# Rolling rows by DMA: the order of the wrapped row ends on GpSimd's ring

## The chip, the cores and the metric

One core of a Trainium2 chip runs the kernel. The metric is the device time of one execution in microseconds (us). The profile is of one execution. Its granted TensorE clock was 1.0, and TensorE does nothing. A run is marked slow when it is over 1.5% above the fastest of the same kernel; with one core and no clock change, that mark only tells how far a run lies from the fastest. Ratios are the mean time of one kernel's fast runs over that of the other's fast runs of the same rounds, so they are not quite the ratio of the medians that are quoted beside them.

## The reference

```python
x = np.random.randn(8192, 8192).astype(np.float32)   # shift = 100
def reference(x, shift):
    return np.roll(x, shift, axis=1)
```

A row has 32 KiB. Of each row, 8,092 elements (32,368 B, "the body") move 100 places to the right, and the last 100 (400 B, "the wrap") go to the front.

## The kernel before

```python
engines = [nc.sync, nc.scalar]
n_chunks = 16
rows = n_rows // n_chunks                  # 512
for i in range(n_chunks):
    r = slice(i * rows, (i + 1) * rows)
    engines[i % 2].dma_start(out=out[r, s:], in_=x[r, :n_cols - s])
    if s > 0:
        nc.gpsimd.dma_start(out=out[r, :s], in_=x[r, n_cols - s:])
# ... launch: one core, x and out in HBM
```

There is no SBUF and no compute: SyncE and ScalarE issue the body in 16 DMAs, GpSimd issues the wraps in 16 DMAs.

## Time and profile before

| | before |
|---|---|
| median of 4 runs | 844.44 us (841.96 to 846.6) |
| wrap packets (queue q0, without completions) | 768, mean 347 ns, 31 over 1 us |
| body packets (q1 and q10) | 8,192, mean 1,590 ns |
| time of all data packets over 16 engines | 830.8 us |
| last packet ends, from the start of the trace | 840.7 us |

The last four rows are from the packet records of the trace. In these records 97.6% of the data packets start within 5 ns of where another one ended, and 16 are under way at once for 750 of the 838.5 us from the first to the last. So I take it that an engine handles one packet at a time without gaps, and the sum of packet times over 16 is then the time that evenly loaded engines would need. The prediction shows the lines of the page.

### The profile page before, as it was taken

To read this page: it belongs to the slowest core of one execution; us is meant where nothing else is said; L and a number is where in the kernel's file an instruction comes from. 1 tells how busy PE (TensorE), PEld (TensorE's weight loads), DVE (VectorE), ACT (ScalarE), POOL (GpSimd) and SP (SyncE) were. 2 spreads that over 40 slices of the span, in tenths; PEclk is the share of its full clock that TensorE was granted. 3 is DMA by queue.
4 is the path that set the end of the run, shared out by engine and by line. 5 is a ranking of instruction groups with operands and counts; after the bars stand their busy time and mean duration, and the time that the engine had idled before them with its cause. 6 is when DMAs were issued, how large, how long until landed. Compare 5 with 4: busy or idle time off the path is not lost. (4 is left out here: it accounts for less than half of the span.)

```text
span 841.9 us, 81 instructions
## 1 busy us (share of the span) xinstructions
POOL 10.2 (1%) x20
## 2 busy tenths in 40 slices
POOL 2000000000000000000000000000000000000000
DMA  9999999999999999999999999999999999999996
GB/s 286 312 315 332 311 322 312 309 315 325 314 332 315 320 321 320 332 326 321 323 323 328 323 321 324 320 321 324 331 328 317 331 324 324 328 332 317 323 331 220
DMA packets 9472, 268.44 MB, mean 319 GB/s; under 512 B 512, under 2 KB 512, under 8 KB 1280
## 3 DMA queue, kind: packets, MB, share of 16 engines
q1 hardware_dynamic: 4224, 132.58, 49.0%
q10 hardware_dynamic: 4224, 132.58, 47.7%
q0 software_dynamic: 1024, 3.28, 2.0%
HBM read 268.44 MB, written 268.44 MB: 638 GB/s over the span
## 5 line engine op out<-in xcount | busy, mean ns | idle before, releaser
L30 POOL DMA_DIRECT2D out_dram<-in_x_dram x16 | 10.0, 630 | 109.5 <-DMA out_dram<-in_x_dram 108.7
L47 POOL MEMSET const-bfloat16-1.0<- 128x1 bf16 x1 | 0.1, 102 | 0.0
L47 POOL MEMSET const-float32-0.0<- 128x1 f32 x1 | 0.1, 99 | 0.2 <-issue 0.2
L47 POOL MEMSET const-float32-1.0<- 128x1 f32 x1 | 0.1, 99 | 0.0
L47 POOL MEMSET const-uint8-127<- 128x1 uint8 x1 | 0.1, 99 | 0.0
## 6 DMA issues: line engine op xcount, KB each, us to landing
out_dram<-in_x_dram ACTq DMA_DIRECT2D x8, 16184.0 KB, 400.1
out_dram<-in_x_dram SPq DMA_DIRECT2D x8, 16184.0 KB, 401.1
out_dram<-in_x_dram POOLq DMA_DIRECT2D x16, 200.0 KB, 112.8
```

Source lines behind the costliest of these rows:

```text
L30: nc.gpsimd.dma_start(out=out[r, :s], in_=x[r, n_cols - s:])
L47: nc = _bacc.Bacc("TRN2", target_bir_lowering=False, num_devices=1)
```

## The change

The intent: consecutive descriptors on GpSimd's ring should not lie on neighbouring rows but 4 rows apart. The body is untouched, and so is the number of wrap DMAs.

```diff
         engines[i % 2].dma_start(out=out[r, s:], in_=x[r, :n_cols - s])
-        if s > 0:
-            nc.gpsimd.dma_start(out=out[r, :s], in_=x[r, n_cols - s:])
+    if s > 0:
+        xt = x.rearrange("(k e m q) c -> k q e m c", k=4, e=16, q=4)
+        ot = out.rearrange("(k e m q) c -> k q e m c", k=4, e=16, q=4)
+        for k in range(4):
+            for q in range(4):
+                nc.gpsimd.dma_start(out=ot[k, q, :, :, :s], in_=xt[k, q, :, :, n_cols - s:])
```

## The prediction

> **What bounds the kernel now.** The kernel only moves bytes: HBM to HBM, 256 MiB read and as much written. So I read the page's second and third parts first, which show how full the 16 DMA engines are and which queue fills them.
>
> ```profile
> span 841.9 us, 81 instructions
> ...
> DMA  9999999999999999999999999999999999999996
> ...
> q1 hardware_dynamic: 4224, 132.58, 49.0%
> q10 hardware_dynamic: 4224, 132.58, 47.7%
> q0 software_dynamic: 1024, 3.28, 2.0%
> HBM read 268.44 MB, written 268.44 MB: 638 GB/s over the span
> ```
>
> The engines are at least nine tenths busy in every slice but the last, where they finish a little apart. The two body queues (SyncE's q1 and ScalarE's q10) take 96.7% of the engines' time, and GpSimd's ring q0, the only thing the change touches, takes 2.0%. That is 0.020 x 842 = 16.8 us of the span for 1.2% of the bytes.
>
> Next I asked whether that 16.8 us is really on the path. The busy time by stretches, with the stretch in which the wraps move (6 to 231 us, from the packet records) and the stretch after it:
>
> ```profile
> core 0: us, POOL busy (x), PEclk, DMA share, GB/s
> 6.00:231.00 225.00, 5.27 (x9) 1.00 1.00 315
> 231.00:820.00 589.00, 0.00 (x0) 1.00 1.00 324
> ```
>
> The engines are full in both (share 1.00), but move 315 GB/s while wraps are mixed in and 324 without. From the packet records: body packets (32,368 B each, 8,192 of them) pass at 9.29 per us in the first stretch and 10.02 per us in the second. So (10.02 - 9.29) x 224.5 = 164 body packets were displaced, which at 10.02 per us is 16.4 us. Two ways of counting agree: the wraps cost about 16.5 us of wall time. The mean duration of a body packet is 1.59 us in both stretches, so wraps take their own time and do not visibly slow the body. If I sort the packets into 16 chains in which each packet starts where another ended, over 95% fit to within 5 ns: an engine handles one packet at a time with no gaps, and the chains end between 831 and 841 us.
>
> Last the waits, to see whether any order between instructions matters:
>
> ```profile
> engine line waited for: us in total, times, longest us
> POOL out_dram L30 <- DMA out_dram<-in_x_dram: 108.7, 8, 15.0
> ```
>
> GpSimd waits 8 times, once for each wrap DMA after the first eight, for an earlier one to land; its last issue is at 119 us and the last wrap packet moves at 231 us. All of it lies 600 us before the end. The instruction chain of the page ends in an unknown queue and names nothing useful here; the bound is the sum of packet times on 16 engines.
>
> [...] The trace shows 512 packets of 4,400 B and 256 of 4,000 B[...] and I expect the same cut after. [...]
>
> **The change part by part.**
> - The body's 16 DMAs keep their queues, order, shapes and rows: 8,192 packets of a mean 1.59 us, 13,025 us of engine time, over 16 engines 814 us. Change: 0.
> - The wraps stay 16 DMAs of 512 x 400 B from GpSimd, 0.63 us of issue each (10.0 us in all, hidden). 768 data packets stay 768. Change in counts: 0.
> - What moves is only the address order. [...] The issue stands behind all body issues in the program text, but GpSimd runs its own stream, so that shifts nothing.
>
> So the whole effect is 768 x (change of a wrap packet's duration) / 16. Today's mean is 267 us / 768 = 347 ns, with a clear shape: 463 of 768 packets (60%) take 185 ns or less, with the fastest at 171 ns for 4,400 B and 155 ns for 4,000 B; the other 40% form a tail up to 1.5 us. If all ran at the fastest: (512 x 171 + 256 x 155) / 16 = 8.0 us. So of 16.7 us, 8.0 us are a floor that no order of rows removes, and 8.7 us are a tail. 171 ns for 4,400 B is 25.7 GB/s on an engine, close to the fastest body packet's 32,368 B / 1,196 ns = 27.1 GB/s. So at 32 KiB pitch a packet can already run at an engine's full pace, and the pitch by itself is not what makes the tail. The tail looks like meeting other traffic: body packets too have a fastest time of 1.20 us and a mean of 1.59. That meeting does not depend on whether the wraps are 1 or 4 rows apart. I choose a mean of 300 to 450 ns after, that is -2.3 to +4.9 us, [...] centre 365 ns, +0.9 us on 845.8.
>
> **Rivals.**
> - *The order removes the tail.* For it: 40% of packets have one, and the change must have been made for something. Against: the floor packets already lie at the same pitch. Best case -8.7 us, 837 us. Even this is 1.0%; 2% (16.9 us) would need wraps that cost nothing.
> - *The pitch hurts.* [...] Against: [...] here in the first 231 us only 1.19 of 16 engines are on a wrap packet at a time (267 / 224.5)[...]. If it doubles the mean to 694 ns: +16.7 us, 862 us, just at 2%. For slower by over 2% the mean must pass 700 ns.
> - *New waits.* The strided pattern of the wraps could be taken by the framework as overlapping the body's writes, and the wraps would wait for body DMAs. The last four (the last 2,048 rows) would then run after the end, one after the other. Against: in before, body and wraps interleave in the same address range too, and no wait between them is in the list, so rows are told apart finely. Estimate 10 to 25 us more, 856 to 870 us. I give it 5%. Waits of wraps for one another alone would be hidden by 600 us of slack.
>
> **Range and chances.** Runs of before spread over 3.5 us. The centre is 846.5 us. The likely band of packet durations gives 843 to 851; the spread of runs, half of the first rival below and a part of the second above widen it to 839 to 857. Faster by over 2% (below 829) has no mechanism: 1%. Slower by over 2% (above 863) needs the doubled packet or new waits: 7%. Within: 92%.
>
> **What would show it.** Right: again 9,472 packets, q0 between 1.7% and 2.6% of the engines' time, body packets at 1.59 us, GB/s about 315 early and 324 late, POOL x16 at about 0.63 us. The tail rival: q0 near 1.0% and nearly all packets under 185 ns. The pitch rival: q0 near 4% and the 171 ns packets gone. New waits: GpSimd waiting hundreds of us, and q0 packets at the end. I am wrong altogether if body packets, which the change does not touch, change their mean duration, or if the wrap DMAs lose engines or are cut into other packets.

## The result, and the profile after

The changed kernel took 869.32 us (median of 4 runs, 865.85 to 884.24; the last is marked slow) beside 844.44. The ratio is 1.0282, with a 95% interval from 1.0223 to 1.0341: slower. The prediction's range ended at 857.

The page of the changed kernel, its span, DMA share by slice, and queues with packets, MB and share of the engines' time:

```profile
span 864.1 us, 81 instructions
...
DMA  9999999999999999999999999999999999999951
...
q10 hardware_dynamic: 4224, 132.58, 46.6%
q1 hardware_dynamic: 4224, 132.58, 46.5%
q0 software_dynamic: 1024, 3.28, 3.5%
```

The numbers of packets and bytes are the same as before. Two things are new. The wraps' share went from 2.0% to 3.5%. And the engines are not full to the end: the last two slices read 5 and 1, where before only the last one read 6. The busy time by stretches shows both (columns: stretch, its length, POOL busy, clock, mean busy share of the DMA engines, GB/s):

```profile
6.00:231.00 225.00, 5.26 (x9) 1.00 1.00 309
231.00:820.00 589.00, 0.00 (x0) 1.00 1.00 323
820.00:864.00 44.00, 0.00 (x0) 1.00 0.41 162
```

The same view of before, for its end:

```profile
820.00:842.00 22.00, 0.00 (x0) 1.00 0.64 224
```

While the wraps move, the kernel is now at 309 GB/s and not 315; afterwards it is as fast as before, 323 beside 324. At the end, the engines are on average only 41% busy for 44 us: some have finished and wait for others.

The packet records give the sum. Wraps: mean 624 ns and not 347, which is 768 x 277 ns / 16 = 13.3 us more. Body: mean 1,572 ns and not 1,590, which is 8,192 x 18 ns / 16 = 9.2 us less. That gain is not spread over the run: from 6 to 231 us, while the wraps move, the body's mean fell from 1,594 to 1,533 ns, after 820 us, when some engines have finished, it is 1,299 and was 1,486, and in between it is as before (1,597 beside 1,592). Body packets ran faster just when other engines were held up by wraps or idle. So the time of all data packets over 16 engines rose from 830.8 to 834.9 us, by 4.1 us only. But the last packet ended at 862.7 us and not 840.7. The gap between the even load and the last engine went from 9.9 to 27.8 us. That is 18 of the 22 us.

When the gap arises is shown by the 4-byte packets. There are 256 of them in the two body queues, 16 for each DMA, and in the trace of before 256 semaphore updates of these DMAs follow them by 0.3 to 1.5 us; so I read them as the reports of completion, one from each engine. For ScalarE's second body DMA the first and last engine reported at 215.3 and 237.0 us before, and at 207.3 and 265.7 us after, a spread of 58 us. Before, the spread at the second DMA was 22 us. In the changed kernel most of it stays to the end: for the last DMA it is 41 us, and was 10 before.

GpSimd's waits are of the same kind as before, so no new order between instructions came in:

```profile
POOL out_dram L36 <- DMA out_dram<-in_x_dram: 126.7, 8, 18.7
```

### The profile page after: what moved, and what is told of

Read it like the earlier page. It is cut to its first block, busy times and chain, and to the rows that moved or that the text cites.

```text
span 864.1 us, 81 instructions
## 1 busy us (share of the span) xinstructions
POOL 10.2 (1%) x20
## 2 busy tenths in 40 slices
DMA packets 9472, 268.44 MB, mean 311 GB/s; under 512 B 512, under 2 KB 512, under 8 KB 1280
## 3 DMA queue, kind: packets, MB, share of 16 engines
q0 software_dynamic: 1024, 3.28, 3.5%
```

## The experiments

Each kernel was timed beside the kernel before on the same chip; before's median on these chips was 841.6 to 851.5 us. Wherever packets are counted below, it is from the packet records of the profiled run. "Long" is a wrap packet over 1 us: 31 of 768 before, 189 after.

The theories in the expectations speak of a pitch "between engines" and one "inside a packet". There I assumed that each of 16 engines takes 32 consecutive rows of a DMA's list. No packet record names its engine or its rows, so this was my assumption and is not shown; the distances in the theories are what I believed. The last section of the experiments comes back to it, because it leaves a riddle. Each diff shows only the lines that matter, against the kernel that they were taken from (before or the changed one), with the omitted lines left out.

### Which part of the order: neighbouring rows in 128-row blocks

```diff
-xt = x.rearrange("(k e m q) c -> k q e m c", k=4, e=16, q=4)          # likewise ot
+xt = x.rearrange("(k e q m) c -> k q e m c", k=4, e=16, q=4, m=32)    # likewise ot
```

> Right result. [...] Theory P (pitch inside a packet): the 128 KiB steps make wrap packets slow; then this runs like before, 842 to 848 us, with a mean wrap packet near 347 ns and engines that end within some 10 us of each other. Theory E (pitch between engines): the 4 MiB between the 16 engines does it; then this runs like the changed kernel, 865 to 872 us, with packets near 620 ns and ends 40 us apart. Theory B (both add): in between, some 855 us and 480 ns.

Measured: 867.02 us, ratio 1.0293 (1.0187 to 1.0398), right result. The time and the ends of the engines (39 us apart) are those of theory E, and the packets are those of theory P: mean 319 ns, 41 long. So it is neither. The stretches of this kernel and of before show a third thing:

```profile
2.00:22.00 20.00, 4.37 (x8) 1.00 1.09 194
22.00:44.00 22.00, 0.63 (x1) 1.00 1.00 227
44.00:120.00 76.00, 3.15 (x5) 1.00 1.00 284
```

```profile
2.00:22.00 20.00, 4.91 (x8) 1.00 1.05 323
22.00:44.00 22.00, 0.62 (x1) 1.00 0.99 307
44.00:120.00 76.00, 3.73 (x6) 1.00 1.00 319
```

The first fence is this kernel, the second is before. Here the body is slowed from the start and recovers over 120 us. The first 16 wrap packets, which leave from 6.3 us on, took 2,445 ns on average (368 before, 1,291 in the changed kernel), and the 32 body packets that started next took 3,730 ns (1,610 before, 1,455 in the changed kernel). This jolt does not exist in the changed kernel. The experiment shows that the same loss of time can come about in two ways, and that a time alone does not tell which.

### No wraps

```diff
-    if s > 0: ...                        # all wrap DMAs removed; wrong result on purpose
```

> Wrong result on purpose: no wraps at all. Gives the cost of the wraps in both kernels. If wraps cost their mean engine time: before minus 16.7 us, about 828 us. If the body alone has its engines level, they end within 5 us of each other, where they ended within 10 us before and 41 us after, and the unevenness is due to the wraps. Rival: the engines are uneven by themselves (20 us or more apart), and the wraps only sum with it.

Measured: 821.09 us, ratio 0.9769 (0.9695 to 0.9842). The wraps cost before 0.0231 x 841.6 = 19.4 us, by the interval 13 to 26, so this agrees with the 16.7 us of their engine time. The body alone leaves the engines 18 us apart at its last DMA, so they are uneven by themselves: my second expectation (5 us) failed, and its rival (20 us or more) is nearly right. But the body's own unevenness grows slowly (5 us at the first DMA, 8 at the second), while the changed kernel has 58 us at the second. Most of the unevenness of the changed kernel comes with the wraps.

### Reads or writes

```diff
+on = out.rearrange("(i e m) c -> i e m c", i=16, e=16)          # neighbouring rows, as before
-... dma_start(out=ot[k, q, :, :, :s], in_=xt[k, q, :, :, n_cols - s:])
+... dma_start(out=on[4 * k + q, :, :, :s], in_=xt[k, q, :, :, n_cols - s:])   # wrong rows on purpose
```

> Wrong rows on purpose: the wraps read in the changed kernel's order and write in the order of before. If the slow side is the reads: about 868 us and wrap packets near 620 ns. If it is the writes: about 845 us and near 350 ns. If each gives half: about 856 us.

Measured: 837.75, 850.53, 864.47 and 877.95 us; only the lowest counts as fast, so there is no ratio. The profiled run is the slowest one: 174 long packets, mean 565 ns, and at the last DMA two engines reported at 873.6 and 874.8 us while the other fourteen were done by 822.8. The end of its DMA line and its wrap queue:

```profile
DMA  9999999999999999999999999999999999998211
...
q0 software_dynamic: 1024, 3.28, 3.1%
```

The long packets are here with the reads alone, and in this run the unevenness too. But the one fast run, at 837.75 us, is no slower than before, and no trace of it was kept. So the effect of the reads alone on the time is not shown.

The mirror, with reads as before and writes in the changed kernel's order:

```diff
+xn = x.rearrange("(i e m) c -> i e m c", i=16, e=16)
+... dma_start(out=ot[k, q, :, :, :s], in_=xn[4 * k + q, :, :, n_cols - s:])   # wrong rows on purpose
```

> Wrong rows on purpose: the wraps read in the order of before and write in the changed kernel's order. The mirror of the run that reads 4 apart: about 868 us and 620 ns if the writes are the slow side, about 845 us and 350 ns if the reads are, about 856 us if each gives half.

Measured: 839.73 us, ratio 1.0025 (0.9921 to 1.0130), mean 343 ns, 17 long. The order of the writes makes no long packets by itself, and no harm to the time is seen (the interval leaves room for 1.3%). The order of the reads makes the long packets.

### The wraps alone, without the body

```diff
-    for i in range(n_chunks): ...        # body removed, wraps kept; wrong result on purpose
```

> Wrong result on purpose: the wraps of before alone, no body. Theory of meeting: a wrap packet is slow only because the body is beside it; then packets run near their floor, 171 ns, in this order and in the changed order alike. Rival: the order is slow by itself; then this shows a mean near 200 ns and the changed order one of 600 ns or more.

> Wrong result on purpose: the changed kernel's wraps alone, no body. Order slow by itself: mean packet over 600 ns, with packets of 1.5 to 3 us as beside the body. Slow only in meeting the body: near 171 ns, the same as the order of before alone.

Measured: 33.35 us in the order of before and 48.53 us in the changed order (one run each). Span and the wraps' queue, first of the order of before, then of the changed one:

```profile
span 31.6 us, 61 instructions
...
q0 software_dynamic: 1024, 3.28, 76.7%
```

```profile
span 46.8 us, 61 instructions
...
q0 software_dynamic: 1024, 3.28, 84.6%
```

The mean packet was 496 ns and 812 ns, with no long packet in the first and 197 in the second. The changed order is slow by itself, with no body to meet: both expectations for the order of before (171 and 200 ns) failed, but the changed order's 600 ns or more came true. It also shows that 171 ns is no typical pace of the old order: with nothing but other wraps beside them, packets took 496 ns on average.

### Is the jolt of the first experiment due to the start?

```diff
+for q in range(4): nc.gpsimd.dma_start(out=ob[0, q, :, :, :s], in_=xb[0, q, :, :, n_cols - s:])   # 128-row blocks
-for i in range(16): ...                  # order of before
+for i in range(4, 16): ...
```

> Right result. [...] Theory of the start: in the run with all sixteen like that, the first round of wrap packets, which all engines send at once at 6.3 us, took 1 to 3 us each and threw the body into packets of 5 us that recover over 120 us; so four such DMAs at the start do all the harm, about 865 us. Rival: the harm goes with the number of such DMAs: 842 + 4/16 x 25, about 848 us.

Measured: 877.97 us, ratio 1.0318 (1.0244 to 1.0391). First 16 wrap packets 2,669 ns, next 32 body packets 3,811 ns. Four such DMAs at the start do as much harm as sixteen. With the four last instead (chunks 0 to 11 in the order of before, then block 3):

> Right result. The mirror: twelve wrap DMAs as before[...]. Theory of the start: like before, 840 to 846 us. Rival (harm by number): about 848 us; if a late collision throws the body too, 855 us or more.

Measured: 859.14 us, ratio 1.0090 (1.0055 to 1.0124), so not free, as the theory of the start had it, but a third of the harm; 848/842 of the rival is 1.007. The start explains most of the first experiment's loss, and not all.

### Reads alone: 4 rows apart at the old block size, and neighbouring rows in blocks of 128

```diff
+src = bass.AP(x.tensor, offset, [[32 * n_cols, 16], [4 * n_cols, 32], [1, s]])   # rows 32e + 4m, wrong rows on purpose
+nc.gpsimd.dma_start(out=on[i, :, :, :s], in_=src)
```

> Wrong rows on purpose: only the wraps' reads differ from before. [...] Theory P (the step inside a packet makes the long packets): 100 or more of the 768 wrap packets over 1 us and a mean near 600 ns, the engines ending 30 us or more apart, ratio to before 1.01 to 1.04. Theory E (only the 4 MiB between engines does it): like before, fewer than 40 packets over 1 us, a mean near 350 ns, ratio 1.00.

Measured: 839.91 us, ratio 0.9885 (0.9844 to 0.9927), mean 309 ns, 23 long. No harm at all, as theory E had it. It reads the same rows several times over, though, which the changed kernel does not.

```diff
+xt = x.rearrange("(k e q m) c -> k q e m c", k=4, e=16, q=4, m=32)
+... dma_start(out=on[4 * k + q, :, :, :s], in_=xt[k, q, :, :, n_cols - s:])   # wrong rows on purpose
```

> Wrong rows on purpose: only the wraps' reads differ from before[...]. If the jolt at the start that the run with this order on both sides showed comes from the reads: first 16 wrap packets over 2 us, body packets of 3 us and more after them, ratio near 1.03. If it needs the writes: first wrap packets under 0.6 us, ratio near 1.00.

Measured: 856.23 us, ratio 1.0078 (1.0047 to 1.0110), mean 573 ns, 159 long. The first 16 wrap packets took 2,559 ns, but the body packets after them only 1,257 ns: with reads alone there is no jolt to the body. Here reads in blocks of 128 rows go with long packets and cost 0.8%. In the first experiment, where the writes lay in the same blocks, only 41 packets were long; why the two differ is open.

### Rows 16 apart, and another cut of the body

```diff
+xt = x.rearrange("(i m e) c -> i e m c", i=16, m=32, e=16)       # likewise ot
```

> Right result. [...] Theory P, where a wider step inside a packet is worse: mean packet over 700 ns, more long packets than the changed kernel, ratio 1.03 or more. Theory E, where engines far apart are the harm: better than before, mean below 347 ns and ratio below 1.00.

Measured: 845.04 us, ratio 0.9956 (0.9925 to 0.9987), mean 353 ns, 26 long. Like before, against both theories.

```diff
+cuts = [(a, a + 496) for a in range(0, 7936, 496)] + [(7936, 8192)]   # body only; wraps as before
```

> Right result. Wraps as before; the body cut into chunks of 496 rows[...]. If body packets are at 1.59 us and not at their fastest 1.20 us because engines 1 MiB apart meet on the same part of memory: a mean below 1.5 us and a ratio below 0.97. If the memory's total rate bounds the body: 1.59 us and ratio 1.00 to 1.02 (the last DMA, 256 rows, leaves one queue short).

Measured: 845.23 us, ratio 0.9996 (0.9962 to 1.0031), body packets 1,584 ns. Nothing is gained. (Chunks of 496 rows make 16 equal shares of 31 rows and not 32. No trace shows which rows an engine takes, so the run does not settle whether the body suffers from distances between its engines.)

### Not exactly 128 rows

```diff
-xt = x.rearrange("(k e m q) c -> k q e m c", k=4, e=16, q=4)
+xt = x[:7936].rearrange("(k e m q) c -> k q e m c", k=4, e=16, q=4)   # m = 31: 124 rows; the last 256 rows in one DMA
```

> Right result. The changed kernel's order [...] with one number altered[...]; the last 256 rows go in one more DMA. Theory E2 (the exact 4 MiB is the harm): [...] mean wrap packet 300 to 360 ns, fewer than 50 packets over 1 us, ratio to before 0.985 to 1.005. Rival (a wide spread or the 4-row order on both sides is the harm): as the changed kernel, 190 packets over 1 us, ratio 1.02 or more.

> The changed kernel itself, on the same chip as the run with 124 rows, to have its ratio beside it: 1.02 to 1.035, with about 190 wrap packets over 1 us and engines that end 30 to 50 us apart.

> Wrong result on purpose: the wraps of the run with 124 rows alone, no body. The same wraps alone took a mean packet of 496 ns in the order of before and 812 ns in the changed order. Theory E2: 500 ns or less. Rival: about 800 ns.

Measured: 876.11 us for the 124 rows, ratio 1.0286 (1.0219 to 1.0352), with 197 long packets of 800; the changed kernel on the same chip 871.27 us, ratio 1.0254 (1.0162 to 1.0346), with 181 long and engines that end 37 us apart; the wraps of the 124 rows alone 47.19 us, mean 751 ns. Theory E2 falls: with 124 in the place of 128 the kernel is as slow. (What distance this makes between two engines is not shown.)

> Right result. The wraps in 64 DMAs of 16 x 8 rows[...]. If the gain of the run that read so (0.9885) is the order's: ratio 0.985 to 0.995, although 1,024 packets of 3,200 B stand for 768. If it came from that run's overlapping reads, or the smaller packets eat it: 0.995 to 1.01.

```diff
+xt = x.rearrange("(i e m q) c -> i q e m c", i=16, e=16, m=8, q=4)   # 64 DMAs of 16 x 8 rows
```

Measured: 868.71 us, ratio 1.0115 (1.0042 to 1.0188), scattered from 856.49 to 887.99, with 217 long packets of 1,024. The gain of the overlapping reads does not appear; the harm of the changed kernel does. (The profiled runs of this kernel, of the one with 124 rows and of the blocks of 129 below were marked slow; their counts of long packets are used here, not their spans.)

### Step of 5, and blocks of 129

```diff
+xt = x[:7680].rearrange("(k e m q) c -> k q e m c", k=3, e=16, m=32, q=5)   # the last 512 rows as before
```

> Right result, 768 data packets as before. The changed kernel's order with the step altered from 4 rows to 5 (160 KiB)[...]; only the last 512 rows as before. If it is the power of two in the step (a packet's rows all of one remainder by four): mean wrap packet 300 to 400 ns, fewer than 50 over 1 us, no long runs of long packets on one engine, ratio 0.99 to 1.01. If any sparse order does it: 150 or more over 1 us, ratio 1.02 or more.

```diff
+xt = x[a:a + 2064].rearrange("(e r) c -> e r c", e=16)               # a = 0, 2064, 4128: three quarters of the rows
+... in_=xt[:, q:128:4, n_cols - s:]                                  # q = 0 .. 3, then row 128 of each; the rest as before
```

> Right result. [...] If the harm is inside a packet: three quarters of the changed kernel's long packets, 140 over 1 us, ratio 1.015 to 1.03. If it is that all engines share one remainder at a time: fewer than 60 over 1 us, ratio 0.99 to 1.01.

Measured: step of 5: 848.10 us, ratio 1.0037 (1.0010 to 1.0063), mean 356 ns, 28 long. Blocks of 129: 842.21 us, ratio 0.9951 (0.9924 to 0.9979), mean 280 ns, 16 long of 816. Their wrap queues, in this order:

```profile
q0 software_dynamic: 1024, 3.28, 2.0%
```

```profile
q0 software_dynamic: 1120, 3.28, 1.7%
```

Both are as before, against 3.5% in the changed kernel. So a sparse order alone does not harm, and neither does any step of 4. Both runs came out as the theory of the power of two had it: that the harm comes when the reads of one DMA lie on rows of one remainder by four.

### One reading of these runs

The step of 4 with blocks of 124 rows is bad, with blocks of 129 it is good. The step of 4 with blocks of 32 is bad with 64 DMAs and good with overlapping reads. Under my assumption of consecutive shares this is a riddle. The trace does record the shape of an instruction's destination: for the changed kernel it gives [512,1] elements of 400 B, one dimension, although the program says 16 x 32. The two dimensions step evenly, and stand there as one. For the blocks of 129, the rows 16 apart and the blocks of 128 on both sides it gives [32,16], two dimensions. For the two runs that only read in another shape (overlapping reads, and reads only in blocks of 128) it gives [1,512]; the shape of the reads is not in the record.

Beside this stands what the program says of the wraps' reads in one DMA, in rows of 32 KiB: the step from one read to the next and, where 16 blocks do not join into one even step, the distance from block to block.

| run | destination in the record | step of the reads, by the program | long packets | ratio |
|---|---|---|---|---|
| before | one dim. | 1 | 31 of 768 | 1 |
| changed kernel | one dim. | 4 | 189 of 768 | 1.0282 |
| reads only, changed order | one dim. | 4 | 174 of 768 | none |
| writes only, changed order | one dim. | 1 | 17 of 768 | 1.0025 |
| 124 rows | one dim. | 4 | 197 of 800 | 1.0286 |
| 64 DMAs | one dim. | 4 | 217 of 1,024 | 1.0115 |
| step of 5 | one dim. | 5 | 28 of 768 | 1.0037 |
| blocks of 129 | two dim. | 4, blocks 129 apart | 16 of 816 | 0.9951 |
| overlapping reads | [1,512] | 4, blocks 32 apart | 23 of 768 | 0.9885 |
| rows 16 apart | two dim. | 16, blocks 1 apart | 26 of 768 | 0.9956 |
| reads only, blocks of 128 | [1,512] | 1, blocks 128 apart | 159 of 768 | 1.0078 |
| reads and writes, blocks of 128 | two dim. | 1, blocks 128 apart | 41 of 768 | 1.0293 |

Every run with an even step of 4 has many long packets (174 to 217), and the run with an even step of 5 has not (28). The two with a step of 4 in blocks that do not join have few (16 and 23). The last two rows have the same reads and yet different counts, so this column does not explain them. "Rows 16 apart" moves the same 512 rows in each DMA as before, in another order, and its packets are like those of before (353 ns and 26 long, beside 347 ns and 31). It still came out 0.4% apart in time. So, by my estimate from this pair, the 0.5% of the blocks of 129 is no proven gain, and no version here beats both kernels beyond doubt.

What this shows and what it doesn't: that the reads in the changed order are slow, with or without the body, is measured, by long packets (174 of 768 beside the body, 197 without it). Which rows one engine or one packet reads is not shown, so no run separates a distance within a packet from one between engines. A second description stands beside the even step of 4, the remainder by four: in each of the runs with an even step of 4 all reads of one such DMA lie on rows of one remainder by four, and in before, the writes-only run, the step of 5, the rows 16 apart and the blocks of 129 they don't. Only the overlapping reads speak against it (one remainder, 23 long), and they read rows several times. No run separates the two. A run with the rows of the changed kernel's DMAs, listed in two dimensions as 16 outer items 4 apart and 32 inner ones 64 apart, would test whether the list or the rows decide; it was not made.

## Why the prediction was wrong

- **The counts were right.** 9,472 packets, the cut of 4,400 and 4,000 B, GpSimd's waits, no order between wraps and body, and a body rate of 323 GB/s after the wraps are as predicted. Body packets changed their mean a little, 1,590 to 1,572 ns, which the prediction named as a sign of being wrong: they ran faster while other engines were held up or idle. Two readings of the old trace were slightly off, with no effect on the result: 446 of 768 wrap packets (58%) took 185 ns or less, and the tail went to 1.59 us.
- **The step that failed first: the mean of 300 to 450 ns.** It rested on "at 32 KiB pitch a packet can already run at an engine's full pace, and the pitch by itself is not what makes the tail", and "the tail looks like meeting other traffic". The wraps alone refute what was concluded from this, that the order does not matter: 496 ns in the old order and 812 ns in the new one, with no body to meet. (That the old order's tail is a meeting of packets is not refuted: the wraps still meet one another there; it is not shown either. And 32 KiB is the pitch of the list; a packet's own pitch is not in the trace.) In the kernel it became 624 ns, +13.3 us where -2.3 to +4.9 was expected. A fast packet beside slow ones did not show that order is harmless; it showed only that some packets went fast.
- **The step that cost most: "the whole effect is 768 x (change of a wrap packet's duration) / 16".** This spreads the cost over all engines. Before, that was nearly right, as the chains ended within 10 us. After, the even load rose by 4.1 us, and the last engine ended 22 us later. By the same division the prediction said that for over 2% slower the mean must pass 700 ns; the kernel was 2.8% slower at 624. The missing term is the unevenness, +18 us. It could not be read off the old trace as a number, but the division by 16 is a claim that the new cost falls evenly, and I did not treat it as one.
- **The rival "the pitch hurts" came nearest, and the reason against it did not hold.** Its signs were q0 near 4%, a mean of 694 ns and the 171 ns packets gone; measured were 3.5%, 624 ns, and 90 packets of 4,400 B at 172 ns or less where before had 216. I held against it that only 1.19 engines are on a wrap at a time. In the changed kernel it is 479 us of packet time over 252 us of wraps, 1.9 engines, because the packets became slow. What pitch an engine's own reads have, before and after, no trace shows.
- **An engine is late by its own wrap packets, as far as packets can be sorted into engines; why it is that engine is open.** Sorted into engines by what starts where another ended (97% fit to 5 ns, but two engines that finish together can be confused), a wrap packet over 700 ns is followed by another on the same engine in 64% of cases in the changed kernel, where 30% of all are that long, and in 22% before, where 14% are. So long packets gather on some engines. In the run that only read in the changed order, a second sorting, which also used the turn of the three queues (in the changed kernel's trace, sorted by ends, a packet of SyncE's queue in the first 240 us was followed by one of ScalarE's in 1,066 of 1,092 cases), follows 14 of the 16 engines to the report of ScalarE's first body DMA: 13 had by then spent 5 to 13 us on wraps and reported at 106 to 115 us, and one had spent 46 us and reported at 152.

## What to carry to other kernels

When engines share a load, read the end of the run by the slowest engine and not by the mean (here the last one ended 27.8 us after the even load, and 9.9 us before the change); the busy share of the last slices shows it at once. A reordering of small DMAs that changes no byte and no count can still cost more than all their data (here 25 us more, where the wraps' whole engine time was 16.7 us), so look at where its reads land, and try another step: here a step of 5 rows in the place of 4 took the harm away (28 long packets and not 189). And when a time matches a theory, check the packets too: here two kernels lost the same 25 us, one by long wrap packets and one by a jolt to the body.
